# Rank indices converted on VectorE, eight score tiles, and three more U products behind the last scores

## The chip, the cores and the metric

One core of a Trainium2 chip runs the kernel. Its engines are TensorE (PE, matrix products), VectorE (DVE), ScalarE (ACT), GpSimd (POOL), and SyncE (SP), which issues most transfers. Each engine runs its own instructions in a fixed order, and waits on semaphores for the others. The metric is the device time of one execution in microseconds (us).

## What is computed

One layer of an encoder on 512 tokens of 1024 features: a mixer (a linear recurrence and a convolution side by side), then a retrieval layer over 128^2 = 16384 experts of one neuron each. The change touches the retrieval:

```python
s = jnp.einsum("thpc,hpkc->thpk", q, sub_keys)        # 8 heads x 2 halves x 128 keys
s1, i1 = lax.top_k(s[:, :, 0], 16)
s2, i2 = lax.top_k(s[:, :, 1], 16)
cand_s = s1[..., :, None] + s2[..., None, :]          # 16 x 16 pairs
top_s, pos = lax.top_k(cand_s, 16)
idx = take_along_axis(i1 * 128 + i2, pos)             # 16 experts for a token and head
gate = softmax(top_s)
act = gelu(einsum("thkd,td->thk", expert_u[idx], xt))
out = einsum("thk,thkd->td", gate * act, expert_v[idx])
```

## The kernel before

For the first 384 tokens (three blocks of 128) the retrieval is computed densely: for each of 128 groups of 128 experts a **U product** (`dense_u`, all experts of the group against the tokens, then gelu), a multiplication with the gates (zero where an expert isn't chosen), and a **V product** that adds into six sums. The last 128 tokens gather their rows instead. Every float32 product is made of three with split operands: ScalarE makes a high part (`split`, L108, `w_hi`), VectorE or GpSimd subtracts it (L110, `w_lo`), and TensorE adds hi*hi, hi*lo and lo*hi. A U product is 24 matmuls of 384 columns (L478 to L480) into one of two buffers `p_e`; ScalarE's gelu (L487) empties it. `w_hi` and `w_lo` have three buffers each, the loaded tiles five.

The stages that matter here, in order:

- **Ranking** (from 277 to 480 us). For each of 16 half heads `hp` a query product (L587 to L589), its copy `q` on ScalarE (L591), the scores `p_s` on TensorE (L602), their copy `s` on ScalarE (L606), and four times `rank` on VectorE (five instructions for the best 16). After heads 1, 3, 5, 6 and 7 `choose` merges: `ii` (L525) converts the indices to bf16, then sums `cs`, the best 16 of them (`ts`, `pos`), `pa` on VectorE, a softmax on GpSimd and ScalarE (L564, L565), `pf` on ScalarE (L545, a conversion of `pa`), and a lookup of the keys by comparison, product and sums (`eq`, L554 to L562). After the scores of `hp` come `US[hp]` U products; their `w_lo` is GpSimd's. One U product runs ahead of all.
- **Scatter** (from 480 to 662 us). `turned` transposes gates and keys of a block (L638, also into `p_e`), then 24 steps of 16 tokens: VectorE builds one-hot tiles `hot` (L661) and `oa` (L665), TensorE multiplies them (L671, 48 small matmuls a step), ScalarE copies (L674, `stg`), SyncE stores to memory (L675). After a step comes a U product whose `w_lo` is VectorE's, while fewer than 46 of them exist.
- **V part** (from 682 us to the end). The gates are loaded back (L740), U products up to 51 are made with `w_lo` on GpSimd (L763), then a loop over 128 groups makes a V product (L777), weighs (L748 to L752), and makes the U product of 47 groups on.

A U product's result stays in a home until its V product: 8 spare tiles, `HOMES_NOW` homes `w_e` that exist during the ranking, others (`w_f`, `w_g`) only later. So a ranking with 15 homes can hold 23 U products: one early and 22 of `US`. The program's order on each engine is set at build time by a scheduler with the buffers in view; it is not the order of the text alone.

Of the kernel before, what the change touches and what calls it, by code (L numbers as in the profile page):

```python
# [8 lines left out]
F32 = mybir.dt.float32  # L9
# [9 lines left out]
P = 128  # L19
T = 512  # L20
D = 1024
NB = T // P
# [4 lines left out]
NK = 128  # L27
# [33 lines left out]
def tile_kernel(ctx, tc, x, par, wi, bd, kd, mg, wo, wq, keys, u_rows, v_rows, u_t, v_t, fg, ffg, sel, out):  # L61
    nc = tc.nc
# [397 lines left out]
    AHEAD_W = 2  # L460
    EARLY = 1

    US = (0, 0, 0, 1, 1, 2, 1, 2, 1, 2, 1, 2, 1, 2, 1, 5)
    us = {}

    HOMES = AHEAD_U + 1 - 8
    HOMES_NOW = 15

    LAG = AHEAD_U - HOMES - 3
    HOMES_END = 3  # L470
# [46 lines left out]
    def choose(rp, v, i, g, keys_, h0, n):  # L517

        hh = slice(h0, h0 + n)
        vv = v[:, hh].rearrange("p h b t k -> p (h b) t k")  # L520
        m = vv.shape[1]
        shp = [P, m, K]

        ii = rp.tile([P, 2, K, m], BF16, name="ii")
        nc.scalar.copy(ii, i[:, hh].rearrange("p h b t k -> p t k (h b)"))  # L525

        cs = rp.tile([P, m, NCD], F32, name="cs", bufs=1)
        for lo_, ni, nj, c0 in ((0, 4, K, 0), (4, 12, 4, 64)):
            (nc.gpsimd if n > 1 else nc.vector).tensor_tensor(
                cs[:, :, c0:c0 + ni * nj].rearrange("p h (i j) -> p h i j", j=nj),  # L530
                vv[:, :, 0, lo_:lo_ + ni].unsqueeze(3).to_broadcast([P, m, ni, nj]),
                vv[:, :, 1, 0:nj].unsqueeze(2).to_broadcast([P, m, ni, nj]), op=ALU.add)
        ts = rp.tile(shp, F32, name="ts")
        pos = rp.tile(shp, U32, name="pos")
        for h in range(m):
            c2 = rp.tile([P, NCD], F32, name="c2")
            best16(ts[:, h], pos[:, h], cs[:, h], c2)

        pa = rp.tile([P, 5, m, K], U32, name="pa")
        for q, (op, arg) in enumerate(((ALU.logical_shift_right, 4), (ALU.logical_shift_right, 2),  # L540
                                       (ALU.bitwise_and, 15), (ALU.bitwise_and, 12),
                                       (ALU.logical_shift_right, 6))):
            nc.vector.tensor_scalar(pa[:, q], pos, arg, None, op0=op)
        pf = rp.tile([P, 5, m, K], F32, name="pf")
        nc.scalar.copy(pf, pa)  # L545
        pb = rp.tile([P, 2, K, m], BF16, name="pb")
        pbm = pb.rearrange("p t k m -> p t m k")
        nc.vector.scalar_tensor_tensor(pbm[:, 0], pf[:, 1], -12.0, pf[:, 0], op0=ALU.add, op1=ALU.max)
        nc.vector.tensor_mul(pf[:, 3], pf[:, 3], pf[:, 4])
        nc.vector.tensor_sub(pbm[:, 1], pf[:, 2], pf[:, 3])  # L550

        eq = rp.tile([P, 2, K, K * m], BF16, name="eq", bufs=1)
        shp2 = [P, 2, K, K * m]
        nc.vector.tensor_tensor(eq, pb.rearrange("p t k m -> p t (k m)").unsqueeze(2).to_broadcast(shp2),  # L554
                                ioj[:, :, 0:K * m].unsqueeze(1).to_broadcast(shp2), op=ALU.is_equal)
        e4 = eq.rearrange("p t j (k m) -> p (t j) k m", m=m)
        nc.vector.tensor_tensor(e4, e4, ii.rearrange("p t j m -> p (t j) m").unsqueeze(2).to_broadcast([P, 2 * K, K, m]),
                                op=ALU.mult)
        for w in (8, 4, 2):
            nc.vector.tensor_add(eq[:, :, 0:w], eq[:, :, 0:w], eq[:, :, w:2 * w])  # L560
        e1, e2 = (eq[:, :, w].rearrange("p t (k m) -> p t k m", m=m) for w in range(2))
        nc.vector.tensor_add(keys_[:, :, hh].rearrange("p t h b k -> p t k (h b)"), e1, e2)  # L562
        g = merge(g[:, hh])
        nc.gpsimd.tensor_tensor(g, ts, ts[:, :, 0:1].to_broadcast(shp), op=ALU.subtract)  # L564
        nc.scalar.activation(g, g, AF.Exp)  # L565
        den = rp.tile([P, m], F32, name="den")
        nc.vector.tensor_reduce(den, g, axis=AX.X, op=ALU.add)
        nc.vector.reciprocal(den, den)
        nc.gpsimd.tensor_tensor(g, g, den.unsqueeze(2).to_broadcast(shp), op=ALU.mult)

    with ExitStack() as rt:
        kp = rt.enter_context(tc.tile_pool(name="kp", bufs=1, side="right"))
        ky = kp.tile([P, 16, NK], F32, name="ky")
        nc.sync.dma_start(ky, keys)
        rp = rt.enter_context(tc.tile_pool(name="rp", bufs=2, side="right"))
        qp = rt.enter_context(tc.tile_pool(name="qp", bufs=4, side="right"))
        ps_q = rt.enter_context(tc.tile_pool(name="ps_q", bufs=3, space=PSUM))
        ps_s = rt.enter_context(tc.tile_pool(name="ps_s", bufs=3, space=PSUM))
        v16 = kp.tile([P, H, NB, 2, K], F32, name="v16")
        i16 = kp.tile([P, H, NB, 2, K], U32, name="i16")  # L580

        def query(hp):
            hi, lo = split(load(wq[hp].rearrange("p c e -> p (c e)")), nc.gpsimd)
            pq = ps_q.tile([P, T], F32, name="pq")
            for c in range(NC):
                cs = slice(c * P, (c + 1) * P)
                nc.tensor.matmul(pq, hi[:, cs], m_hi[:, c, :], start=(c == 0), stop=False)  # L587
                nc.tensor.matmul(pq, hi[:, cs], m_lo[:, c, :], start=False, stop=False)  # L588
                nc.tensor.matmul(pq, lo[:, cs], m_hi[:, c, :], start=False, stop=(c == NC - 1))  # L589
            q = qp.tile([P, T], F32, name="q", bufs=2)  # L590
            nc.scalar.activation(q, pq, AF.Copy)  # L591
            return q

        for _ in range(EARLY):
            dense_u(len(us), nc.gpsimd)
        qs = [query(0)]
        for hp in range(16):
            if 0 < hp < 15:
                qs.append(query(hp + 1))
            p = ps_s.tile([P, NB, NK], F32, name="p_s")  # L600
            for b in range(NB):
                nc.tensor.matmul(p[:, b, :], qs[hp][:, b * P:(b + 1) * P], ky[:, hp, :], start=True, stop=True)  # L602
            if hp == 0:
                qs.append(query(1))
            s = qp.tile([P, NB, NK], F32, name="s")
            nc.scalar.activation(s, p, AF.Copy)  # L606
            for b in range(NB):
                rank(rp, v16[:, hp // 2, b, hp % 2], i16[:, hp // 2, b, hp % 2], s[:, b])
            for _ in range(US[hp]):
                dense_u(len(us), nc.gpsimd)  # L610
            for h0, n in ((0, 2), (2, 2), (4, 2), (6, 1), (7, 1)):
                if hp == 2 * (h0 + n) - 1:
                    choose(rp, v16, i16, gate_d, key_d, h0, n)
        nc.vector.scalar_tensor_tensor(eidx, key_d[:, 0, :, DB], float(NK), key_d[:, 1, :, DB], op0=ALU.mult, op1=ALU.add)
# [278 lines left out]
```

## Time and profile before

| | |
|---|---|
| median of 3 runs | 1543.34 us (1542.52 to 1551.58) |
| the profiled execution | 1543.64 us, span 1541.5 us |
| TensorE busy | 95% of the span |
| VectorE busy | 80% |
| ScalarE, GpSimd busy | 41% each |
| granted TensorE clock, mean | 0.978 of full speed |
| DMA queue of the loads | 222 MB, 42% of 16 engines' time |

The span is counted from the first to the last instruction; the 2.1 us around it are in the execution's time. Busy shares are means over stages with different limits. In a row of the timeline stand the start, the duration, the engine, the line, the operation, output and inputs, and in brackets the idle time before it and what ended that.

### The profile page before, as it was taken

How to read it: one execution, taken by the hardware profiler on the slowest of the kernel's cores; microseconds unless marked ns; L12 is line 12 of the kernel's file. 1: busy time of each engine (PE TensorE's matmuls, PEld its weight loads, DVE VectorE, ACT ScalarE, POOL GpSimd, SP SyncE). 2: the span in 40 equal slices, each digit the busy share in tenths (PEclk: the TensorE clock that was granted, in tenths of full speed). 3: DMA queues.
4: the chain of work that ended last, by engine and by line, in shares of the span. 5: the costliest groups of instructions: out<-in, count | busy, mean ns of one | idle time of the engine just before them, and what ended most of it. 6: DMA issues, size and time to landing. Idle time of an engine off the chain costs nothing.

```text
span 1541.5 us, 21654 instructions
## 1 busy us (share of the span) xinstructions
PE 1467.7 (95%) x7939; PEld 1289.4 (84%) x7939; DVE 1232.5 (80%) x2267; ACT 626.7 (41%) x926; POOL 625.4 (41%) x378
## 2 busy tenths in 40 slices
PE   5998698999988999999999999999999999999997
PEld 4766467899977899898999999999999999888886
DVE  5998556599999999937777777777777778788887
ACT  5457633344434555433333333333333333333333
POOL 1636542467551000124545545544454444443330
PEclk8999899999998999999999999999999999999999
DMA  6211313233222665588899898999989899889983
GB/s 238 82 55 58 134 69 123 97 109 98 92 95 100 226 212 213 212 259 311 290 334 318 327 340 289 342 305 332 326 318 326 301 348 319 304 310 339 331 290 135
DMA packets 137787, 358.69 MB, mean 233 GB/s; under 512 B 10064, under 2 KB 59472, under 8 KB 134352
## 3 DMA queue, kind: packets, MB, share of 16 engines
q1 hardware_dynamic: 100240, 222.03, 42.0%
q0 software_dynamic: 36864, 134.23, 24.2%
q8 instruction: 62, 1.02, 0.3%
q10 hardware_dynamic: 576, 1.05, 0.2%
q14 instruction: 45, 0.37, 0.1%
HBM read 327.91 MB, written 29.36 MB: 232 GB/s over the span
## 4 chain that ended last, share of the span: by engine, by line
PE 81%; DVE 13%; ACT 3%; issue 1%; POOL 1%; DMA 0%; SPq 0%; DVEq 0%; ACTq 0%; POOLq 0%
PE po L777 34%; PE p_e L478 10%; PE p_e L479 10%; PE p_e L480 10%; PE p_g L671 3%; DVE oa L665 2%; PE pq L587 2%; PE pq L588 2%; PE pq L589 2%; DVE hot L661 1%; PE pz L432 1%; PE pz L431 1%; PE pz L433 1%; PE pz L339 1%; PE pz L340 1%
## 5 line engine op out<-in xcount | busy, mean ns | idle before, releaser
L108 ACT CAST w_hi<-raw_t 128x1024 fp32r<-128x1024 f32 x302 | 315.9, 1050 | 411.6 <-PE p_e L479 266.8
L478 PE MATMUL p_e<-m_hi,w_hi 128*128 128x384 f32 x1024 | 350.7, 342 | 4.4 <-ACT w_e L487 3.5
L480 PE MATMUL p_e<-m_hi,w_lo 128*128 128x384 f32 x1024 | 347.3, 339 | 0.0
L479 PE MATMUL p_e<-m_lo,w_hi 128*128 128x384 f32 x1024 | 346.8, 339 | 0.3 <-DVE m_lo L142 0.3
L110 POOL TENSOR_TENSOR w_lo<-raw_t,w_hi 128x1024 fp32r<-128x1024 f32 x70 | 189.8, 2720 | 349.2 <-ACT w_hi L108 349.2
L110 DVE TENSOR_TENSOR w_lo<-raw_t,w_hi 128x1024 fp32r<-128x1024 f32 x232 | 280.9, 1222 | 13.6 <-ACT w_hi L108 13.4
L693 POOL DMA_INDIRECT g_t<-in_u_rows,eidx x128 | 197.4, 1543 | 214.0 <-DVE g_t L705 170.2
L693 POOL DMA_INDIRECT g_t<-in_v_rows,eidx x128 | 178.7, 1396 | 234.8 <-DVE acc L715 222.1
L777 PE MATMUL po<-w_hi,wt_hi 128*128 128x512 f32 x768 | 240.6, 393 | 0.0
L777 PE MATMUL po<-w_hi,wt_lo 128*128 128x512 f32 x768 | 239.5, 391 | 0.0
L777 PE MATMUL po<-w_lo,wt_hi 128*128 128x512 f32 x768 | 238.8, 390 | 0.0
L478 PEld LDWEIGHTS p_e<-m_hi,w_hi 128*128 128x128 f32 x1024 | 194.5, 190 | 8.3 <-ACT w_e L487 3.9
L479 PEld LDWEIGHTS p_e<-m_lo,w_hi 128*128 128x128 f32 x1024 | 194.5, 190 | 3.5 <-DVE m_lo L142 0.5
L480 PEld LDWEIGHTS p_e<-m_hi,w_lo 128*128 128x128 f32 x1024 | 194.5, 190 | 0.0
L777 PEld LDWEIGHTS po<-w_lo,wt_hi 128*128 128x128 f32 x768 | 144.2, 188 | 32.9
L777 PEld LDWEIGHTS po<-w_hi,wt_lo 128*128 128x128 f32 x768 | 144.3, 188 | 30.5
L705 DVE SCALAR_TENSOR_TENSOR g_t<-g_t,Xg 128x1024 f32<-128x1024 f32 x128 | 152.0, 1222 | 19.0 <-DMA g_t<-in_u_rows,eidx 18.8
L777 PEld LDWEIGHTS po<-w_hi,wt_hi 128*128 128x128 f32 x768 | 143.2, 188 | 24.9
L715 DVE SCALAR_TENSOR_TENSOR acc<-g_t,dots,acc 128x1024 f32<-128x1024 f32 x127 | 162.5, 1279 | 1.7 <-DMA g_t<-in_v_rows,eidx 1.7
L750 ACT CAST wt_hi<-w_f 128x384 fp32r<-128x384 f32 x69 | 35.4, 513 | 182.1 <-PE po L777 182.1
L752 DVE TENSOR_TENSOR wt_lo<-w_f,wt_hi 128x384 fp32r<-128x384 f32 x69 | 38.5, 558 | 73.7 <-ACT wt_hi L750 73.6
L665 DVE TENSOR_TENSOR oa<-hot,trb 128x1024 bf16<-128x1024 bf16 x144 | 92.3, 699 | 0.6
(220 smaller groups left out, 1906.2 us busy)
## 6 DMA issues: line engine op xcount, KB each, us to landing
raw_t<-in_u_t SPq DMA_DIRECT2D x128, 512.0 KB, 6.1
raw_t<-in_v_t SPq DMA_DIRECT2D x128, 512.0 KB, 6.1
scr_g<-stg SPq DMA_DIRECT2D x24, 1024.0 KB, 4.8
g_s<-scr_g SPq DMA_DIRECT2D x16, 1536.0 KB, 14.6
raw_t<-in_wi SPq DMA_DIRECT2D x16, 512.0 KB, 4.2
raw_t<-in_wq SPq DMA_DIRECT2D x16, 512.0 KB, 3.6
raw_t<-in_wo SPq DMA_DIRECT2D x8, 512.0 KB, 3.6
raw_t<-in_kd SPq DMA_DIRECT2D x6, 512.0 KB, 3.5
```

The source lines that it names most:

```text
L108: nc.scalar.copy(hi, t)
L110: eng.tensor_sub(lo, t, f(hi))
L478: nc.tensor.matmul(p, hi[:, cs], m_hi[:, c, :TD], start=(c == 0), stop=False)
L479: nc.tensor.matmul(p, hi[:, cs], m_lo[:, c, :TD], start=False, stop=False)
L480: nc.tensor.matmul(p, lo[:, cs], m_hi[:, c, :TD], start=False, stop=(c == NC - 1))
L665: nc.vector.tensor_tensor(oa[:, q], hot[:, 1], over(2 + q, 1), op=ALU.mult)
L671: nc.tensor.matmul(p[:, t, :], hot[:, 0, g, :, o], oa[:, q, g, :, o], start=(q == 0), stop=(q == 2))
L693: nc.gpsimd.indirect_dma_start(out=t, out_offset=None, in_=rows, in_offset=bass.IndirectOffsetOnAxis(ap=eidx[:, k // K, k % K:k % K + 1], ...
L705: nc.vector.scalar_tensor_tensor(t, t, 1.0, Xg, op0=ALU.mult, op1=ALU.mult, accum_out=dots[:, k:k + 1])
L715: nc.vector.scalar_tensor_tensor(acc, t, dots[:, k:k + 1], acc, op0=ALU.mult, op1=ALU.add)
L752: weighed.append(nc.vector.tensor_sub(wlo, flat(w), f(whi)))
L777: nc.tensor.matmul(po[b][hf], lhs[:, bs], rhs[:, hf * 512:(hf + 1) * 512], start=(i == 0 and n == 0), stop=(i == NK - 1 and n == 2))
```

## The change

Three edits. The conversion of the indices `ii` in `choose` goes from ScalarE to VectorE (five instructions). The score tiles `s` have eight buffers, not four. And `US` puts eight U products behind the scores of the last half head, not five, with 18 homes in the ranking instead of 15 (and 23 `w_f` instead of 26, since `wk2` gets `HOMES - HOMES_NOW - HOMES_END`). As the scatter makes U products up to 46 in all, it then makes 20 and not 23, and its last four steps have none, where the last one had none before.

```diff
-    US = (0, 0, 0, 1, 1, 2, 1, 2, 1, 2, 1, 2, 1, 2, 1, 5)
+    US = (0, 0, 0, 1, 1, 2, 1, 2, 1, 2, 1, 2, 1, 2, 1, 8)
...
-    HOMES_NOW = 15
+    HOMES_NOW = 18
...
-        nc.scalar.copy(ii, i[:, hh].rearrange("p h b t k -> p t k (h b)"))
+        nc.vector.tensor_copy(ii, i[:, hh].rearrange("p h b t k -> p t k (h b)"))
...
-            s = qp.tile([P, NB, NK], F32, name="s")
+            s = qp.tile([P, NB, NK], F32, name="s", bufs=8)
```

What it does to the engines' order is seen at three places. First ScalarE, from the copy of the last scores (`s`) to the gelu of the third product behind them. The products are told apart by the number of their `p_e`: 3818, 3851, 3884 and so on are the first, second and third. Before:

```order
L606 ACTIVATE s_3786<-p_s_3781 128x512
L108 CAST w_hi_3913<-raw_t_3911 128x1024
L487 ACTIVATE w_e_3843<-p_e_3818 128x384
L525 CAST ii_3977<-i16_1905 128x128
L108 CAST w_hi_3946<-raw_t_3944 128x1024
L487 ACTIVATE w_e_3876<-p_e_3851 128x384
L565 ACT_TABLE_LOAD
L565 ACTIVATE gate_d_65<-gate_d_65 128x64
L545 CAST pf_4014<-pa_4008 128x320
L487 ACT_TABLE_LOAD
L487 ACTIVATE w_e_3909<-p_e_3884 128x384
```

And now:

```order
L606 ACTIVATE s_3786<-p_s_3781 128x512
L108 CAST w_hi_3913<-raw_t_3911 128x1024
L487 ACTIVATE w_e_3843<-p_e_3818 128x384
L108 CAST w_hi_3946<-raw_t_3944 128x1024
L487 ACTIVATE w_e_3876<-p_e_3851 128x384
L565 ACT_TABLE_LOAD
L565 ACTIVATE gate_d_65<-gate_d_65 128x64
L545 CAST pf_4113<-pa_4107 128x320
L487 ACT_TABLE_LOAD
L487 ACTIVATE w_e_3909<-p_e_3884 128x384
```

Only `ii` has left; the exponential and `pf` stand where they stood, ahead of the third product's gelu. The merge before this one differs in the same way: there `ii` leaves, and `pf` stays ahead of the copy of the last query.

Second TensorE, at the transposes with which the scatter begins. Before, they follow the fifth product behind the last scores (`p_e_3950`), and the first product of the scatter follows them:

```order
L478 MATMUL p_e_3950<-m_hi_70,w_hi_3946 128x384
L479 MATMUL p_e_3950<-m_lo_71,w_hi_3946 128x384
L480 MATMUL p_e_3950<-m_hi_70,w_lo_3948 128x384
L638 MATMUL p_e_4053<-ident_58,src_4054 128x128
L638 MATMUL p_e_4058<-ident_58,src_4059 128x128
L638 MATMUL p_e_4063<-ident_58,src_4064 128x128
L478 MATMUL p_e_4149<-m_hi_70,w_hi_4145 128x384
```

Now they follow the eighth (`p_e_4049`):

```order
L478 MATMUL p_e_4049<-m_hi_70,w_hi_4045 128x384
L479 MATMUL p_e_4049<-m_lo_71,w_hi_4045 128x384
L480 MATMUL p_e_4049<-m_hi_70,w_lo_4047 128x384
L638 MATMUL p_e_4152<-ident_58,src_4153 128x128
L638 MATMUL p_e_4157<-ident_58,src_4158 128x128
L638 MATMUL p_e_4162<-ident_58,src_4163 128x128
L478 MATMUL p_e_4248<-m_hi_70,w_hi_4244 128x384
```

So 72 matmuls have come between the last scores and the transposes.

Third TensorE at the end of the scatter, around the last small matmul into `p_g_6541`. The five products that follow the scatter (made for homes 47 to 51) write `p_e_6576`, `6609`, `6642`, `6675` and `6708`. Before, all five, 120 matmuls, stand behind it:

```order
L671 MATMUL p_g_6541<-oa_6523,hot_6521 128x128
L671 LDWEIGHTS hot_6521
L671 MATMUL p_g_6541<-oa_6523,hot_6521 128x128
L478 MATMUL p_e_6576<-m_hi_70,w_hi_6572 128x384
L479 MATMUL p_e_6576<-m_lo_71,w_hi_6572 128x384
```

Now the first two and three matmuls of the third have moved in among the last scatter steps, and 69 are left behind it:

```order
L671 MATMUL p_g_6541<-oa_6523,hot_6521 128x128
L671 LDWEIGHTS hot_6521
L671 MATMUL p_g_6541<-oa_6523,hot_6521 128x128
L478 MATMUL p_e_6642<-m_hi_70,w_hi_6638 128x384
L479 MATMUL p_e_6642<-m_lo_71,w_hi_6638 128x384
```

From the first V product on, TensorE's order is the same in both.

## Rows read from the trace of the kernel before

**Rows 1.** Windows: length, busy (instructions) of each engine, clock, DMA share, GB/s.
```profile
440.00:460.00 20.00, 12.61 (x63) 12.29 (x62) 19.47 (x81) 10.30 (x15) 11.70 (x6) 0.83 0.24 80
...
620.00:640.00 20.00, 20.00 (x204) 19.68 (x201) 20.00 (x26) 9.63 (x18) 0.00 (x0) 1.00 0.59 221
```

**Rows 2.** Waits, TensorE and ScalarE, 400 to 480 us: total, times, longest.
```profile
PE p_s L602 <- ACT q L591: 7.4, 1, 7.4
PE p_e L478 <- ACT w_e L487: 3.5, 1, 3.5
...
ACT ii L525 <- DVE i L508: 22.4, 3, 13.1
ACT w_hi L108 <- issue: 12.0, 4, 3.7
ACT gate_d L565 <- POOL gate_d L564: 9.1, 3, 5.0
ACT w_hi L108 <- PE p_e L479: 1.5, 1, 1.5
ACT pf L545 <- DVE pa L543: 1.2, 3, 0.4
```

**Rows 3.** Timeline of ScalarE at the last two merges.
```profile
447.32 0.46 ACT L545 CAST pf<-pa 128x320 f32<-128x320 uint32 x1 [0.39 <-DVE pa L543]
...
448.63 0.59 ACT L591 ACTIVATE q<-pq 128x512 f32<-128x512 f32 x1
...
474.31 0.49 ACT L487 ACTIVATE w_e<-p_e 128x384 f32<-128x384 f32 x1
```

**Rows 4.** Timeline of TensorE from the last scores to the transposes.
```profile
449.27 2.07 PE L602 MATMUL p_s<-ky,q 128*128 128x128 f32 x8 [7.39 <-ACT q L591]
...
456.01 0.33 PE L478 MATMUL p_e<-m_hi,w_hi 128*128 128x384 f32 x1
...
456.53 0.33 PE L478 MATMUL p_e<-m_hi,w_hi 128*128 128x384 f32 x1
...
464.68 0.34 PE L480 MATMUL p_e<-m_hi,w_lo 128*128 128x384 f32 x1
468.56 0.69 PE L478 MATMUL p_e<-m_hi,w_hi 128*128 128x384 f32 x1 [3.55 <-ACT w_e L487]
...
480.75 0.33 PE L638 MATMUL p_e<-ident,src 128*128 128x128 f32 x1 [0.95 <-ACT src L637]
```

**Rows 5.** Timeline of VectorE: a key, a sum, the scatter.
```profile
432.50 0.58 DVE L562 TENSOR_TENSOR key_d<-eq 128x256 f32<-128x256 bf16 x1
...
441.50 0.41 DVE L529 TENSOR_TENSOR cs<-v 128x256 f32<-128x256 f32 x1
...
484.06 2.36 DVE L661 TENSOR_TENSOR hot<-iot,trb 128x2048 bf16<-128x2048 bf16 x2 [0.24 <-ACT trb L639]
...
641.75 3.22 DVE L661 TENSOR_TENSOR hot<-iot,trb 128x2048 bf16<-128x2048 bf16 x1
...
652.04 1.21 DVE L661 TENSOR_TENSOR hot<-iot,trb 128x2048 bf16<-128x2048 bf16 x1
...
656.35 1.89 DVE L665 TENSOR_TENSOR oa<-hot,trb 128x1024 bf16<-128x1024 bf16 x3
```

**Rows 6.** Groups of VectorE, 484 to 659 us: busy, mean ns, idle before.
```profile
L110 DVE TENSOR_TENSOR w_lo<-raw_t,w_hi 128x1024 fp32r<-128x1024 f32 x20 | 24.4, 1218 | 1.5 <-ACT w_hi L108 1.5
```

**Rows 7.** Timeline of GpSimd at the scatter's end.
```profile
641.31 2.58 POOL L110 TENSOR_TENSOR w_lo<-raw_t,w_hi 128x1024 fp32r<-128x1024 f32 x1 [159.34 <-ACT w_hi L108]
```

**Rows 8.** Timeline of ScalarE, VectorE and TensorE from the scatter to V.
```profile
660.39 2.21 ACT L674 ACTIVATE stg<-p_g 128x512 f32<-128x512 f32 x4
...
678.73 0.98 ACT L750 CAST wt_hi<-g_t 128x384 fp32r<-128x384 f32 x2 [2.89 <-DVE g_t L748]
...
678.14 1.03 DVE L748 TENSOR_TENSOR g_t<-g_t,g_s 128x384 f32<-128x384 f32 x2 [19.90 <-DMA g_s<-scr_g]
...
682.66 0.62 PE L777 MATMUL po<-w_hi,wt_hi 128*128 128x512 f32 x2
```

## The prediction

> **What bounds the kernel now.** I read the table of windows first, then the waits, then the rows in order of time around the stretch that the change touches. TensorE is the busiest engine (95% in the table), but not everywhere. From 440 to 460 us it works 12.61 of 20 us while VectorE works 19.47 [rows 1]: at the end of the ranking VectorE sets the pace. In the scatter both are full (20.00 and 20.00 of 20 us) [rows 1].
>
> The waits of TensorE and ScalarE from 400 to 480 us show why TensorE starves [rows 2]. ScalarE waits 22.4 us in all for indices of VectorE (the conversion `ii`), the longest time 13.1 us. TensorE waits twice, 7.4 us for the query `q` of the last scores and 3.5 us for a gelu `w_e`. The rows in time order show what really stands ahead of each. `q` runs at 448.63, behind `pf` at 447.32, and `pf` waits for VectorE's merge as `ii` does [rows 2, 3]. Taking `ii` away leaves `pf`. The last scores start at 449.27 [rows 4]. In what follows product 1 to 5 (after the change 1 to 8) are the U products behind them.
>
> **The conversions on VectorE.** Five go over. No row shows a VectorE conversion of this kind. From below it costs nothing (it could fit where VectorE waits); from above, the nearest row is the 128x256 sum `cs` at 0.41 us [rows 5], so 2 us for five. The three large ones lie well ahead; I take two small ones of 0.3 us on the path, 0.6 us, since they follow `cs` directly in the last two merges. ScalarE gains what it no longer waits: in its order the conversion of product 1's U tile now stands ahead of the first wait and the gelu of product 2 ahead of the second. The first gives TensorE nothing, because its instructions run in order and the last scores, which come first, still wait for `q`. The second lets product 4 run without its wait.
>
> **Eight tiles of scores.** Four more buffers are worth something only where ScalarE waits for a free one. Among ScalarE's waits there is none of that kind [rows 2], and the order does not change. I cost it at nothing; if VectorE fell further behind, it would be cover.
>
> **Three more products behind the last scores.** A product is 24 matmuls; three start every 0.52 us [rows 4], so 4.16 us. Before, products 1 to 3 end at 465.02 [rows 4]; product 4 then waits 3.55 us for a free buffer of sums, that is for the gelu of product 2. It and product 5 take from 468.56 to 479.80 (0.95 us ahead of the first transpose), 11.24 us instead of 8.32, at a lower clock (the granted clock from 440 to 460 us, around the first of these waits, is 0.83 of full speed [rows 1], between the levels of 1.2 and 2.4 GHz): 2.9 us lost. The three transposes of the scatter start at 480.75 [rows 4].
>
> After: product 4 runs from 465.0 to 469.2. Product 5 needs the gelu of product 3, which stands behind the second `pf` and ends at 474.80 [rows 3]; with the 0.6 us, product 5 starts at 475.4. The wait has not gone, it has moved by one product and grown to 6 us. At the clock seen in product 4 it takes 4.16 + 2.9 = 7.1 us, to 482.5; products 6 to 8 take 12.5 us, to 495.0. Then the transposes start: 495.0 against 480.75, **14.25 us later**. VectorE, whose ranks are done by about 481 (before, the first transpose followed them at 480.75), waits for them: its first one-hot comes 3.3 us behind the first transpose, as before (484.06 [rows 5]), at 498.3.
>
> **What the scatter gives back.** VectorE sets its pace: from 484.06 to the end of the last `oa` at 658.24 [rows 5] are 174.2 us, with 20 subtractions `w_lo` of 1.22 us [rows 6]. Three go: 3.7 us less. Against that stand the products after the scatter, whose `w_lo` GpSimd does. A one-hot that meets one takes 3.22 us, not 1.21 [rows 5], and there the two started within 0.5 us of each other [rows 7]. Before, two such subtractions fall into VectorE's work. After, the last five products begin among the last scatter steps, and with three buffers of weights four of the five `w_lo` fall in: two more, 4.0 us. So VectorE needs 174.5 us and ends at 672.8.
>
> The Trainium skill (SBUF — State Buffer, section "SBUF: two separate sides") has a rule for this: GpSimd and a VectorE instruction with two inputs in SBUF hold a shared pair of ports for a whole instruction, and the other blocks. By that rule the trace agrees: the one-hot ended 1.1 us after GpSimd's instruction. Priced as full blocking by that instruction's 2.58 us the two would cost 5.2 instead of 4.0 us.
>
> **The way to the first V product.** Before, the last scatter tile is copied by 662.60, the gates come back from memory at 678.14, and the first V matmul starts at 682.66, after five products that fill the time [rows 8]. It could have started at 679.3: the first of two weights, converted from 678.73 in 0.98 us, is then done [rows 8], 16.7 us behind the copy. After, only 69 of 120 matmuls are left behind the last scatter matmul. VectorE's end at 672.8, 1.2 us of matmuls and 0.6 us of copy give 674.6; 16.7 us more give 691.3. TensorE has run out of products at 674.0 + 12.0 = 686.0 and waits 5.3 us. So the V products start at 691.3 against 682.66, 8.6 us later, and at the lower clock: after its wait of 7.39 us the last scores and three products took 15.75 us (449.27 to 465.02), some 2.2 above their time, after 3.55 us two took 2.9 more; I take 2.5. From there TensorE's order is the same as before and TensorE is full, so that the end moves as much.
>
> Two small terms: the `w_lo` of product 1 now runs just when VectorE forms a key (432.50, [rows 5]), 0 to 2.0 us, and the queue that loads the gates has one more tile load ahead of it that waits for a subtraction, 0 to 1.5 us. I take 1.0 and 0.5.
>
> Sum: 8.6 + 2.5 + 1.0 + 0.5 = **+12.6 us**. The profiled execution took 1543.64 us (span 1541.5), 0.3 above the median of 1543.34. That gives 1556.2; I say **1556**.
>
> In short: the change is (delay of the transposes) + 0.3 - 2.5 - 3.4 + 2.5, and small terms. The 2.5 taken off is that the last scatter matmuls no longer queue behind a product (copy's end +12.0 against VectorE's +14.5), the 3.4 is the slack of the gates (679.3 against 682.66). It breaks even where the transposes are about 3 us late, at 484.
>
> **Rivals.**
> 1. *The three products fill idle time.* If product 5 does not wait for `pf`, products 4 to 8 end at 465.0 + 20.8 = 485.8, the transposes are 5.1 us late and the sum is about +2: 1546. For it speaks that TensorE is idle 11 us in this stretch [rows 2]; against it that ScalarE's order keeps both `pf` ahead of what TensorE needs. Chance 0.10.
> 2. *Not slower: the last scores come early.* If `q` is no longer held, they start when the query is done, about 442, and if the second `pf` holds nothing either, eight products end before 480. Then the transposes wait for the last key only and are not late: -3 us, 1540.5. The point that decides is whether `pf` still stands ahead of `q`; it does. More than 3 us cannot be gained here, since the ranks end at 480 by VectorE. Chance 0.05.
> 3. *More collisions of GpSimd and VectorE.* The key meets `w_lo` fully (+1.0), a fifth `w_lo` falls into the scatter's end (+2.0), the five conversions cost their upper bound on the path (+1.4), the load queue its 1.5 (+1.0), the clock 2.9 (+0.4): +18.4, 1562. The rule cited above would go this way. For it speaks the 3.22 us row; against it that most of these are races. Chance 0.25.
> 4. The forecast, 0.60, by itself 1551 to 1560.
>
> **Numbers.** Within 1% of 1543.3 (15.4 us), about what a measurement of this kernel can tell from no change, lie rivals 1 and 2, most of the forecast and a little of rival 3. Slower by over 1% (above 1558.8): nine tenths of rival 3 (0.22) and the upper part of the forecast (0.11), 0.33. Faster by over 1% needs the transposes 12 us earlier, before the ranks they need exist: 0.02. Same: 0.65. The range reaches from rival 1's side to rival 3: 1545 to 1563.
>
> **What would show it.** In the new profile: the last scores still start at 449 to 452, behind `pf`; TensorE waits for a gelu of about 6 us near 469; the first transpose starts near 495 and VectorE is idle from about 481 to 498 but for three subtractions; the last `oa` ends near 673; TensorE waits some 5 us for the first weights and V starts near 692. I am wrong if the transposes start before 484 (then no loss), if the scatter is more than 3 us shorter than 174, or if the V products run faster than before.

## The result, and the profile after

The changed kernel takes **1561.61 us** (median of 6 runs, 1559.30 to 1562.46) against 1544.30 us of the kernel before in the same comparison (1542.52 to 1551.58). The ratio is **1.0107, 95% interval 1.0092 to 1.0123**: slower by some 17 us, on the edge of the 1% beyond which the prediction called a difference slower. The profiled execution took 1562.46 us with a span of 1560.7 us. The median lies within the predicted range (1545 to 1563), and 5.6 us above the predicted 1556.

Windows of the changed kernel: length, busy time and instructions of TensorE's matmuls, of its weight loads, VectorE, ScalarE and GpSimd, then granted clock, DMA share, GB/s. They answer to [rows 1].

```profile
440.00:460.00 20.00, 10.28 (x51) 9.96 (x50) 19.51 (x91) 5.84 (x9) 6.72 (x4) 0.74 0.09 29
...
620.00:640.00 20.00, 20.00 (x212) 19.53 (x211) 19.88 (x24) 10.50 (x18) 2.52 (x1) 1.00 0.53 204
...
680.00:700.00 20.00, 12.35 (x70) 12.03 (x70) 5.03 (x6) 5.82 (x10) 1.56 (x1) 0.87 0.79 236
700.00:720.00 20.00, 20.00 (x80) 16.38 (x80) 10.09 (x17) 6.54 (x10) 3.20 (x3) 0.88 0.70 224
```

At the end of the ranking TensorE works even less than before (10.28 of 20 us against 12.61), and a new hole has opened at 680 to 700 us, where it works 12.35 us.

Waits of the changed kernel, 400 to 480 us (total, times, longest), to be read beside [rows 2]:

```profile
ACT gate_d L565 <- POOL gate_d L564: 28.7, 3, 15.0
...
PE p_s L602 <- ACT q L591: 9.7, 1, 9.7
...
PE p_e L478 <- ACT w_e L487: 5.5, 1, 5.5
```

ScalarE's 22.4 us of waits for `ii` are gone. In their place it waits 28.7 us for the softmax of the same merges (9.1 us before). TensorE waits longer than before, for the same two tiles. The rows in time order, of ScalarE and then of TensorE, answer to [rows 3, 4]:

```profile
451.68 0.26 ACT L565 ACTIVATE gate_d<-gate_d 128x64 f32<-128x64 f32 x1 [15.04 <-POOL gate_d L564]
452.33 0.46 ACT L545 CAST pf<-pa 128x320 f32<-128x320 uint32 x1 [0.39 <-DVE pa L543]
...
453.64 0.59 ACT L591 ACTIVATE q<-pq 128x512 f32<-128x512 f32 x1
...
476.91 0.26 ACT L565 ACTIVATE gate_d<-gate_d 128x64 f32<-128x64 f32 x1 [8.23 <-POOL gate_d L564]
...
479.33 0.49 ACT L487 ACTIVATE w_e<-p_e 128x384 f32<-128x384 f32 x1
```

```profile
454.28 2.08 PE L602 MATMUL p_s<-ky,q 128*128 128x128 f32 x8 [9.72 <-ACT q L591]
...
479.87 0.69 PE L478 MATMUL p_e<-m_hi,w_hi 128*128 128x384 f32 x1 [5.51 <-ACT w_e L487]
...
498.10 0.27 PE L638 MATMUL p_e<-ident,src 128*128 128x128 f32 x1
```

`q` still stands behind `pf`; the wait for a gelu has moved from product 4 to product 5 (479.87); the transposes start at 498.10 instead of 480.75. VectorE starts its first one-hot at 501.57 (484.06 before [rows 5]) and ends its last `oa` at 678.42 (658.24):

```profile
501.57 2.36 DVE L661 TENSOR_TENSOR hot<-iot,trb 128x2048 bf16<-128x2048 bf16 x2 [0.20 <-ACT trb L639]
...
676.52 1.90 DVE L665 TENSOR_TENSOR oa<-hot,trb 128x1024 bf16<-128x1024 bf16 x3
```

On the way to the first V product, in the order of engines SyncE (its queue), VectorE, TensorE, beside [rows 8]:

```profile
681.59 0.33 SPq L103 DMA_DIRECT2D raw_t<-in_u_t  x1
682.01 0.38 SPq L675 DMA_DIRECT2D scr_g<-stg  x1
...
688.59 6.21 SPq L740 DMA_DIRECT2D g_s<-scr_g  x2
```

```profile
698.54 1.03 DVE L748 TENSOR_TENSOR g_t<-g_t,g_s 128x384 f32<-128x384 f32 x2 [4.29 <-DMA g_s<-scr_g]
```

```profile
699.69 1.22 PE L777 MATMUL po<-w_hi,wt_hi 128*128 128x512 f32 x2 [7.65 <-ACT wt_hi L750]
```

V starts 17.0 us later than before (682.66), and TensorE stands idle for 7.65 us ahead of it. The span grew by 19.2 us in these two executions; 1.84 us of that were there already at the first scores (276.65 and 278.49), ahead of all that the change touches. In the twelve kernels below the first scores lie between 275.58 and 278.89 whatever the edit, so this is taken as a difference between executions (from the first scores on, the two differ by 17.4 us, and the medians by 17.3). Times are given from the first scores where a microsecond matters.

### The profile page after: what moved, and what is told of

Same layout as the page of the kernel before. It is cut to its first block, busy times and chain, and to the rows that moved or that the text cites. A ratio compares the mean times of both kernels' runs of the same rounds, so it can differ in the third digit from the quotient of the medians.

```text
span 1560.7 us, 21647 instructions
## 1 busy us (share of the span) xinstructions
PE 1470.5 (94%) x7939; PEld 1287.0 (82%) x7939; DVE 1244.1 (80%) x2269; ACT 624.9 (40%) x921; POOL 634.6 (41%) x381
## 4 chain that ended last, share of the span: by engine, by line
PE 71%; DVE 22%; ACT 3%; DMA 1%; issue 1%; POOL 1%; SPq 0%; DVEq 0%; ACTq 0%; POOLq 0%
PE po L777 34%; PE p_e L478 9%; PE p_e L479 8%; PE p_e L480 8%; PE p_g L671 2%; DVE oa L665 2%; DVE hot L661 2%; DVE eq L560 2%; PE pz L432 1%; DVE eq L557 1%; PE pz L433 1%; PE pz L431 1%; DVE i L508 1%; DVE s L506 1%; DVE i L505 1%
## 5 line engine op out<-in xcount | busy, mean ns | idle before, releaser
L110 POOL TENSOR_TENSOR w_lo<-raw_t,w_hi 128x1024 fp32r<-128x1024 f32 x73 | 198.0, 2725 | 331.7 <-ACT w_hi L108 320.0
L750 ACT CAST wt_hi<-w_f 128x384 fp32r<-128x384 f32 x60 | 30.8, 513 | 157.6 <-PE po L777 157.6
L665 DVE TENSOR_TENSOR oa<-hot,trb 128x1024 bf16<-128x1024 bf16 x144 | 92.7, 701 | 0.8
L671 PE MATMUL p_g<-oa,hot 128*128 128x128 bf16 x1152 | 82.8, 222 | 6.5 <-DVE oa L665 6.1
```

The source lines that it names most:

```text
L110: eng.tensor_sub(lo, t, f(hi))
L665: nc.vector.tensor_tensor(oa[:, q], hot[:, 1], over(2 + q, 1), op=ALU.mult)
L671: nc.tensor.matmul(p[:, t, :], hot[:, 0, g, :, o], oa[:, q, g, :, o], start=(q == 0), stop=(q == 2))
```

## The experiments

Theory A, the prediction's: three products behind the last scores are paid for, because ScalarE's row holds `q` and then a gelu behind a merge. The rivals asked how much belongs to the conversions, and how much to GpSimd and VectorE meeting. "Before" in a ratio is the kernel before, run beside.

### e1_ii_only: the conversions alone

```
-        nc.scalar.copy(ii, i[:, hh]...)
+        nc.vector.tensor_copy(ii, i[:, hh]...)      # the kernel before, otherwise
```

> The kernel before with one edit: the five conversions ii go from ScalarE to VectorE. The prediction costed this at +0.6 us on the last scores and 0 to 2 us for one key that meets a subtraction of GpSimd, so 1543 to 1546 us. Theory A, from the trace of the changed kernel (three large conversions of 0.96 us, three keys of 2.5 to 2.8 us where before two of them took 0.6): the last scores start 3 to 5 us later than 449.27, so at 452 to 454, the transposes as much later, and the time is 1546 to 1549. Rival B: the later scores of the changed kernel (1.84 us of them there already ahead of the first ranking) have nothing to do with ii, and ScalarE's freed time lets product 4 run without its 3.55 us wait: last scores at 449 to 450, transposes up to 3 us earlier, 1540 to 1543.

Measured: 1546.12 us, ratio 1.0015 (1.0002 to 1.0028). VectorE at the third merge, then TensorE:

```profile
434.12 2.52 DVE L562 TENSOR_TENSOR key_d<-eq 128x256 f32<-128x256 bf16 x1
```

```profile
452.88 2.07 PE L602 MATMUL p_s<-ky,q 128*128 128x128 f32 x8 [9.75 <-ACT q L591]
...
478.47 0.69 PE L478 MATMUL p_e<-m_hi,w_hi 128*128 128x384 f32 x1 [5.55 <-ACT w_e L487]
```

Theory A holds: the last scores come 175.8 us behind the first ones, 3.2 later than before, just as in the changed kernel. The conversions themselves take 0.97 us each in the three large merges, where 0.41 was the upper bound taken, and cost next to nothing: VectorE no longer waits 0.78 us there for GpSimd's sums, and from the first scores `pf` of the first merge is only 0.14 us later. What costs is the key behind it: it takes 2.82, 2.52 and 2.52 us, and before 0.59, 2.69 and 0.58. It now falls into a row of GpSimd's `w_lo` each time (the third of them ends at 436.17, the key at 436.64). The wait of product 4 is gone, product 5 waits 5.55 us, as it does in the changed kernel; with five products that wait is still there.

### e2_s8_only: eight tiles of scores alone

```
-            s = qp.tile([P, NB, NK], F32, name="s")
+            s = qp.tile([P, NB, NK], F32, name="s", bufs=8)
```

> The kernel before with one edit: eight tiles of scores instead of four. Prediction: nothing, 1542 to 1546 us, the scores and the transposes at the same times to 0.5 us. Rival: the scores run further ahead of VectorE, so that ScalarE reaches pf and q in another order of time or the stretch ahead of the ranking is 1.8 us longer as in the changed kernel; then the first scores start at 278.5 instead of 276.65 and the time is about 1545 to 1547.

Measured: 1544.53 us, ratio 1.0006 (0.9991 to 1.0021). From the first scores (275.58) the last ones stand at 172.6 and the first transpose at 204.1, as before. Nothing, as predicted.

### e3_products_only: three more products alone

```
-    US = (..., 1, 2, 1, 5)        HOMES_NOW = 15
+    US = (..., 1, 2, 1, 8)        HOMES_NOW = 18
```

> The kernel before with one edit: three more U products behind the last scores (eight instead of five, 18 homes in the first part). Theory A: nearly the whole loss is here. The last scores stay at 449.3, the wait for the second pf moves behind product 4 and grows, and the transposes start 12 to 15 us later than 480.75, at 493 to 496. By the prediction's way from there (2.5 and 3.4 us given back, 2.5 lost to the clock) 1553 to 1556; by what the changed kernel showed (the delay passed on in full, and 2.5 for the clock) 1556 to 1560. Rival B: without ii on VectorE the three products fit the idle time better, the transposes are less than 8 us late, 1546 to 1551, and the rest of the loss belongs to the conversions.

Measured: 1557.62 us, ratio 1.0082 (1.0047 to 1.0117). TensorE:

```profile
449.51 2.08 PE L602 MATMUL p_s<-ky,q 128*128 128x128 f32 x8 [7.40 <-ACT q L591]
...
468.82 0.69 PE L478 MATMUL p_e<-m_hi,w_hi 128*128 128x384 f32 x1 [3.54 <-ACT w_e L487]
...
492.82 0.27 PE L638 MATMUL p_e<-ident,src 128*128 128x128 f32 x1
```

By the ratios, three quarters of the loss are here. The detail of theory A is wrong for this kernel: with `ii` on ScalarE the wait stays at product 4 (3.54 us). The three products follow 4 and 5 in one piece, and the transposes come 11.8 us later from the first scores; that is the whole cost up to there. The three single edits sum to 1.0015 + 1.0006 + 1.0082, 1.03% in all; the whole change is 1.07%.

### e4_early: the three products ahead of the last scores

```
-    US = (..., 1, 2, 1, 8)        # the changed kernel
+    US = (..., 1, 2, 4, 5)
```

> The changed kernel with one edit: the three extra U products stand ahead of the last scores (four instead of one there) and five behind, as before. Theory A (where a product stands decides; ahead of the last scores TensorE is idle 9.7 us for q): the last scores start some 4 to 6 us later than 454.28, at 458 to 460, behind them five products with the wait of 3 to 6 us, and the transposes start at 489 to 494 instead of 498.1: 1552 to 1558. Rival B: q is held by pf all the same, ScalarE has the gelus of the three products in its row behind pf, so that nothing fills the idle time: transposes at 497 or later, 1560 to 1564.

Measured: 1559.36 us, ratio 1.0087 (1.0054 to 1.0119), whose interval overlaps that of the changed kernel. The transposes start at 492.17, 3.9 us earlier from the first scores, so far as A says. But the last scores start at 466.24, not 458 to 460: the third product ahead of them waits 8.79 us for a gelu (at 455.49), since that gelu stands behind `pf` too. The gain is gone before V: the scatter took 178.8 us (1.9 more) and the way from its last `oa` to V another 2.0 more, and V starts 421.3 us behind the first scores (421.2 in the changed kernel). In time this is inconclusive.

### e7_free: nothing of the merge in ScalarE's way

```
-        nc.scalar.copy(pf, pa)
+        (nc.scalar.copy if n > 1 else nc.vector.tensor_copy)(pf, pa)
...
+        if h0 == 6:
+            return
+        if h0 == 7:
+            hh, ts, m = slice(6, 8), both[0], 2 * m
...
+        with tc.issue_after(gelus[-3].ins) if h0 == 7 else ExitStack():
             nc.scalar.activation(g, g, AF.Exp)
```

(`both` holds `ts` of the last two merges, which get one softmax; `gelus` lists the gelus of the U products; `issue_after` places an instruction behind another in its engine's order.)

> The changed kernel with what held q and the gelus taken out of ScalarE's row: in the last two merges VectorE converts pf itself, and the softmax of both is done once, behind the last merge, its Exp placed behind the gelu of product 6. Theory A (pf and Exp ahead of q and of a gelu are the whole reason why the eight products cost their full time): the last scores start at 442 to 447 instead of 454.28, no wait of TensorE for a gelu over 2 us, the transposes at 482 to 487 instead of 498.1, and since that delay is passed on in full, 1544 to 1551 us. Rival B (the products cost their time wherever they stand, or the clock or the loads hold them): transposes at 493 or later, 1556 to 1561.

Measured: 1562.07 us, ratio 1.0123 (1.0108 to 1.0139). TensorE, then GpSimd (the numbers of lines have moved):

```profile
443.88 1.05 PE L616 MATMUL p_s<-ky,q 128*128 128x128 f32 x8
...
476.53 0.69 PE L481 MATMUL p_e<-m_hi,w_lo 128*128 128x384 f32 x1 [14.61 <-POOL w_lo L110]
```

```profile
450.13 2.40 POOL L110 TENSOR_TENSOR w_lo<-raw_t,w_hi 128x1024 fp32r<-128x1024 f32 x1 [2.40 <-ACT w_hi L108]
473.75 0.40 POOL L577 TENSOR_TENSOR gate_d<-ts 128x128 f32<-128x128 f32 x1 [21.22 <-DVE ts L508]
474.10 7.14 POOL L110 TENSOR_TENSOR w_lo<-raw_t,w_hi 128x1024 fp32r<-128x1024 f32 x3
```

Half of A holds: with `pf` and the Exp out of the way `q` runs at once and the last scores start at 443.88 with no wait. The other half fails: all that was won is lost in one wait of 14.61 us for a `w_lo`, which stands in GpSimd's row behind the softmax's subtraction, and that waits 21.22 us for VectorE's merge. The merge had held the products in two engines; freeing one shows the other. The transposes (495.74, 1.9 us earlier from the first scores) and the time are nearly those of the changed kernel, as rival B's numbers said, though the products did not cost "wherever they stand".

### e7b_free5: the same with five products

```
-    US = (..., 1, 2, 1, 8)        HOMES_NOW = 18        # e7_free; Exp behind the gelu of the last product
+    US = (..., 1, 2, 1, 5)        HOMES_NOW = 15
```

> As e7_free, with five products behind the last scores and 15 homes as before (Exp behind the gelu of product 5). The ranks and keys of VectorE then set the transposes: 480 to 484, TensorE idle 8 to 12 us ahead of them in one piece. 1541 to 1548 us: no gain over the kernel before worth more than 0.2%. Rival (idle time of TensorE ahead of the transposes costs, and it costs more in one piece than in two): 1548 to 1552.

Measured: 1547.95 us, ratio 1.0034 (1.0021 to 1.0047). The same wait stands in product 4 (14.60 us, ending at 475.47), and the transposes wait another 4.44 us for the gates, whose Exp stands behind the last gelu: 486.72 instead of 480 to 484. Slower than before, by GpSimd's row again; the question that this run was to answer, what one long idle time costs, stays open.

### e8_vec: the subtractions behind the scatter on VectorE

```
     while len(us) < AHEAD_U:
-        dense_u(len(us), nc.gpsimd)        # the changed kernel
+        dense_u(len(us), nc.vector)
```

> The changed kernel with one edit: the subtractions w_lo of the five U products that follow the scatter are made by VectorE, not GpSimd. Four of them met a hot or oa of VectorE in the changed kernel (3.0 to 4.0 us instead of 1.2 or less, 8.9 us together) and the last one held a load and with it the last store of the gates by 1.0 us. Theory A (these meetings are why the scatter did not get shorter by its three subtractions): the scatter takes 172 to 174.5 us instead of 176.85, the V products start 3 to 5 us earlier relative to the transposes, 1556 to 1559 us. Rival B (the meetings fall where VectorE had time to spare, TensorE sets the scatter's pace): scatter 176 or more, 1560 to 1563 us.

Measured: **1550.86 us, ratio 1.0059** (1.0044 to 1.0073), against 1.0107 for the changed kernel: well below what A expected. The scatter takes 170.5 us instead of 176.85. To see why, the end of the scatter in the changed kernel, first VectorE, then GpSimd, then TensorE (beside [rows 5, 7]):

```profile
636.91 3.22 DVE L661 TENSOR_TENSOR hot<-iot,trb 128x2048 bf16<-128x2048 bf16 x1
...
655.78 3.03 DVE L661 TENSOR_TENSOR hot<-iot,trb 128x2048 bf16<-128x2048 bf16 x1 [2.37 <-PE p_g L671]
...
670.00 3.42 DVE L661 TENSOR_TENSOR hot<-iot,trb 128x2048 bf16<-128x2048 bf16 x1
```

```profile
636.53 2.52 POOL L110 TENSOR_TENSOR w_lo<-raw_t,w_hi 128x1024 fp32r<-128x1024 f32 x1 [144.77 <-ACT w_hi L108]
...
655.34 2.39 POOL L110 TENSOR_TENSOR w_lo<-raw_t,w_hi 128x1024 fp32r<-128x1024 f32 x1 [9.21 <-ACT w_hi L108]
669.38 2.95 POOL L110 TENSOR_TENSOR w_lo<-raw_t,w_hi 128x1024 fp32r<-128x1024 f32 x1 [11.65 <-PE p_g L671]
```

```profile
646.73 0.22 PE L671 MATMUL p_g<-oa,hot 128*128 128x128 bf16 x1 [2.52 <-DVE oa L665]
...
659.59 0.29 PE L671 MATMUL p_g<-oa,hot 128*128 128x128 bf16 x2 [1.90 <-DVE oa L665]
```

A one-hot that meets a `w_lo` takes 2 us more; TensorE then waits for `oa`; and later VectorE waits 2.37 us for TensorE, which is to give back a tile. The delay is paid twice. The kernel before has one such wait of VectorE for TensorE in its scatter, at the start and not behind a meeting:

```profile
491.14 1.23 DVE L661 TENSOR_TENSOR hot<-iot,trb 128x2048 bf16<-128x2048 bf16 x1 [1.11 <-PE p_g L671]
```

In e8_vec none of these rows is left: TensorE waits 1.2 us for `oa` in the whole scatter (6.1 in the changed kernel, 3.7 before), and its clock from 640 to 680 us is 1.00 instead of 0.91.

The shorter scatter is 6.3 us of a gain that, from the first scores, amounts to 10.6 at the start of V. The rest, 4.3 us, lies between the last copy and V, in SyncE's queue:

```profile
668.55 0.33 SPq L103 DMA_DIRECT2D raw_t<-in_u_t  x1
672.65 0.32 SPq L675 DMA_DIRECT2D scr_g<-stg  x1
...
676.56 5.35 SPq L740 DMA_DIRECT2D g_s<-scr_g  x2
```

The last store of the gates is issued 0.03 us behind its copy; in the changed kernel it came 1.4 us behind it (0.4 before), after a load that waited for a buffer which GpSimd held. And from that store to the first reading of the gates 3.9 us pass, instead of 6.6. In all nine traces here with a tile load issued within 1 us ahead of that store, the kernel before among them, this takes 6.6 to 7.0 us; in the five where the last load was issued 4.1 us ahead it takes 3.9. No run moves the load alone, so that the load is the cause is not shown.

### e9_free_vec: both

```
     e7_free and e8_vec together
```

> e7_free and e8_vec together. If both theories A hold and the two gains add: transposes at 482 to 487, scatter 172 to 174.5, and 1539 to 1547 us, 3 to 5 us below e7_free. If the scatter's end is set by TensorE once its products come earlier: as e7_free, 1544 to 1551.

Measured: 1550.33 us, ratio 1.0043 (1.0030 to 1.0056): e8_vec within the intervals. The wait for GpSimd is there as in e7_free (14.59 us), so e7's edit adds nothing here either; the gain of e8_vec does not need it.

### e10_all_free: the last softmax off GpSimd

```
-        nc.gpsimd.tensor_tensor(g, ts, ...)        # e9_free_vec; the product g * 1/den likewise
+        (nc.gpsimd if n > 1 else nc.vector).tensor_tensor(g, ts, ...)
```

> e9_free_vec with one edit: the subtraction and the product of the last softmax go from GpSimd to VectorE. In e7_free the last scores started at 443.88 as theory A wanted, but product 4 then waited 14.6 us for its w_lo, which stood on GpSimd behind the softmax's subtraction (that waited 21.2 us for ts of VectorE). Theory A (each engine whose row holds a step of the merge ahead of a step of the products makes TensorE wait; free all three and the products fill the idle time): no wait of TensorE over 2 us between the last scores and product 8, transposes at 480 to 486 instead of 493.5, scatter 171 to 173 us, 1535 to 1542 us, so faster than the kernel before. Rival B (GpSimd's subtractions, now running through the last ranks, slow VectorE and so move the keys): last key at 486 or later, transposes 488 or later, 1543 to 1548.

Measured: 1546.81 us, ratio 1.0019 (1.0010 to 1.0028). Its windows at the end of the ranking, then TensorE's first transpose:

```profile
440.00:460.00 20.00, 20.00 (x122) 20.00 (x122) 19.66 (x91) 8.01 (x12) 10.42 (x5) 1.00 0.35 114
460.00:480.00 20.00, 19.14 (x111) 18.82 (x109) 19.80 (x97) 5.59 (x7) 6.99 (x3) 1.00 0.27 87
```

```profile
492.81 0.48 PE L653 MATMUL p_e<-ident,src 128*128 128x128 f32 x1 [13.66 <-ACT w_e L488]
```

The products now fill the idle time: no wait from the last scores to 479.1, where product 8 ends, and a full clock. That much of A is shown. But the transposes still come at 492.81. They need the buffer of sums that the gelu of product 8 empties, and that gelu stands on ScalarE behind the copy of the gates, which waits 7.95 us for VectorE's product of the softmax; this one was placed behind the last key and a `w_lo`. Rival B's numbers fit, its mechanism only in part: the last key is 1.7 us later from the first scores than in the changed kernel, and one of the last two keys meets a `w_lo` (2.58 us instead of 0.38).

### e11_ii_large_act: the large conversions back

```
-        nc.vector.tensor_copy(ii, ...)        # e10_all_free
+        (nc.scalar.copy if n > 1 else nc.vector.tensor_copy)(ii, ...)
```

> e10_all_free with the three large conversions ii back on ScalarE (the two small ones stay on VectorE). By e1_ii_only the conversions on VectorE cost 3.2 us at the last scores. Theory A: the last scores start 2.5 to 3.5 us earlier than in e10_all_free relative to the first ones, the transposes 1 to 3.5 us earlier, 1 to 3.5 us less time in all. Rival B (ScalarE waits longer, holds a gelu again and gives it back to TensorE's waits): no difference from e10_all_free beyond 1 us, or slower.

Measured: 1545.81 us, ratio 1.0014 (1.0005 to 1.0023). From the first scores the last ones come 0.84 us earlier than in e10_all_free, and so does the transpose: less than A wanted. Two of the three large keys meet a `w_lo` here too (2.69 us), since GpSimd's subtractions stand elsewhere than before. So the 3.2 us of e1_ii_only belong, by these rows, less to the conversion than to the places where keys and subtractions come to lie.

### e12_before_vec: the same step of e8 in the kernel before

```
     while len(us) < AHEAD_U:
-        dense_u(len(us), nc.gpsimd)        # the kernel before
+        dense_u(len(us), nc.vector)
```

> The kernel before with one edit: the w_lo of the five U products behind the scatter on VectorE instead of GpSimd (as e8_vec, without the change). Two of them met VectorE's work in the kernel before. Theory A (there TensorE set the way to the first V product: it had products to run until 682.8, 3.4 us past the gates): the scatter is 2 to 4 us shorter, the V products gain no more than 1 us, 1542 to 1545 us. Rival B (the scatter's end decides in both kernels): 1538 to 1541 us.

Measured: **1538.87 us, ratio 0.9971** (0.9959 to 0.9983): faster than both kernels, and A, which took most of the price of the two meetings in the kernel before for hidden, is wrong. Waits of TensorE, 480 to 680 us, then the window in which the meetings lie, each time first of the kernel before and then of this one:

```profile
PE p_g L671 <- DVE oa L665: 3.7, 5, 2.5
```

```profile
PE p_g L671 <- DVE oa L665: 0.8, 3, 0.3
```

```profile
640.00:660.00 20.00, 17.01 (x163) 16.12 (x163) 18.00 (x19) 8.04 (x13) 5.22 (x2) 0.91 0.49 176
```

```profile
640.00:660.00 20.00, 20.00 (x212) 19.53 (x211) 17.10 (x23) 10.48 (x18) 0.00 (x0) 1.00 0.59 216
```

The scatter is 2.5 us shorter and V starts at 678.14 instead of 682.66. From the scatter to V TensorE is full in both kernels, and V waits for its products, as A said; the gates, ready at 672.83, are not what V waits for. But in the kernel before TensorE was late with them, because within the scatter it had waited 2.51 us for one `oa` and had run at a clock of 0.91 from 640 to 660 us. So rival B's time came out, by TensorE's row and not by the scatter's end alone.

### e13_row: three places in the rows

```
-        with tc.issue_after(gelus[-3].ins) if h0 == 7 else ExitStack():
+        with tc.issue_after(gelus[-1].ins) if h0 == 7 else ExitStack():
             nc.scalar.activation(g, g, AF.Exp)
...
+        with tc.issue_after(done.ins) if done else ExitStack():
             last = nc.vector.tensor_add(keys_[:, :, hh].rearrange("p t h b k -> p t k (h b)"), e1, e2)
...
+        with tc.issue_after(last_key[0].ins) if last_key and eng is nc.vector else ExitStack():
             eng.tensor_sub(lo, t, f(hi))
```

(`done` is the softmax's product of the last merge, `last_key` its key.)

> e11_ii_large_act with three places in a row put right. There the eight products ran without a wait, but the transposes stood behind the gelu of product 8, that behind the copy of the gates, and that behind VectorE's product of the softmax, which was placed behind the last key and a w_lo. Now the Exp stands behind the gelu of product 8, the softmax's product ahead of the last key, and VectorE's first w_lo behind that key. Theory A (the rows of the engines are what is left): the first transpose follows the last scores by 42 to 45 us instead of 48.0, so at 482 to 486 when the first scores start near 276, the first one-hot 3 to 5 us earlier relative to the first scores, and the time is 1539 to 1543 us, below e11_ii_large_act and not above the kernel before. Rival B (VectorE's own work from the last scores to the key sets it): first one-hot as in e11_ii_large_act to 1 us, 1544 to 1547.

Measured: 1542.10 us, ratio 0.9990 (0.9981 to 0.9999). TensorE:

```profile
485.89 0.47 PE L660 MATMUL p_e<-ident,src 128*128 128x128 f32 x1 [9.34 <-ACT src L659]
```

A holds in all its numbers: the first transpose 43.7 us behind the last scores, the first one-hot 4.5 us earlier from the first scores than in e11_ii_large_act, and eight products behind the last scores that cost nothing. They gain next to nothing either (0.1%): TensorE idles 9.34 us ahead of the transposes, now for VectorE's merge alone, the bound that rival 2 of the prediction named. It idles another 5.47 us ahead of V (680.00), where it was full in the kernel before: the products that fill one hole are missing in later ones. This kernel has e8's edit in it, which gives the kernel before 0.3% by itself (e12_before_vec): against that, three more products behind the last scores are no gain even where they cost no time of their own.

## Why the prediction was right, and where it was off

The sign, the mechanism and the place were right; the size fell short. Of the signs named, the last `oa` (678.42 instead of 673) and the start of V (699.69 instead of 692) came later than said. The way from the first scores to the end, predicted and measured as differences between after and before:

| step | predicted | measured |
|---|---|---|
| up to the first scores | 0 | +1.84 |
| first scores to last scores | +1.6 | +3.17 |
| last scores to transposes | +13.65 | +12.34 |
| transposes to the first one-hot | 0 | +0.16 |
| scatter on VectorE | +0.3 | +2.67 |
| last `oa` to the last copy | -2.5 | -2.15 |
| last copy to the first V | -2.9 | -1.00 |
| V start to the end of the span | +2.5 | +2.17 |
| sum | +12.65 | +19.20 |

- **The conversions and the keys** (0.6 on the path, and 1.0 for one key). Mis-sized: 3.17, and nearly all of it by keys. That a key meets a `w_lo` was foreseen for one key; two more do than before (e1_ii_only). The 0.41 us taken as the upper bound of a conversion was wrong too (0.96 for the large ones), yet mostly hidden.
- **Eight tiles of scores**: nothing, and e2_s8_only shows it.
- **Three products ahead of the transposes**: right. The wait moved to product 5 and took 5.51 us (6 predicted), and the last scores with four products ran 454.28 to 474.36. The four products behind the wait took 18.2 us, where 19.6 had been taken (granted clock 0.92 from 480 to 500 us; in the kernel before 0.83 from 460 to 480). Without the conversions, e3_products_only, the same three cost 11.8 us without the wait moving. That `pf` stands ahead of `q` and decides was the point on which rival 2 hung; e7_free shows it, and that the same merge sits in GpSimd's row as well, which the prediction did not look at.
- **The scatter** (174.5 us). Mis-sized: 176.85. Four subtractions fell into it, as predicted, and the two additional ones cost 4.7 us where 4.0 was taken (the one-hots together 64.0 us, before 59.7; the `oa` 92.7 and 92.3). The step that failed is "VectorE sets its pace": TensorE, held by the late `oa`, held VectorE in turn for 2.37 us. The kernel before had one such wait, of 1.11 us at the scatter's start, which the changed kernel has not. So this added 1.3 us, and with the 0.7 of the meetings that is 2.0 of the 2.4 us missed. e8_vec removes both, and the scatter falls by 6.3 us, though VectorE makes five more subtractions in it.
- **The slack of the gates** (3.4 us given back, 0.5 for the load queue). Only 1.0 was given back. The store was issued 1.4 us behind its copy (0.4 before), for the queue, and the gates took 9.95 us to be read, where they had taken 8.41. Why the reading took longer is not settled: in e8_vec it took 9.7 and in e12_before_vec 7.9.
- **The clock of V** (2.5 us): right. The first 72 matmuls of V took 19.17 us against 16.64 before, and the end came 2.17 us later than V's start alone makes it.

So what happened is the forecast's mechanism with much of rival 3, more meetings of GpSimd and VectorE, on top: keys, scatter and the way of the gates make up 1.6 + 2.4 + 1.9 = 5.9 of the 6.6 us missed (1.5 of them the slower reading, whose cause is open); the rest is the 1.84 ahead of the change, less 1.1 that the other steps together came out lower. Rival 3 gave 1562, and named the keys and the load queue; the wait of VectorE for TensorE was in neither. That the time fell on its number is in part luck, since its fifth `w_lo` in the scatter did not come, nor its 2.9 us of clock. The Trainium skill (SBUF — State Buffer, section "SBUF: two separate sides"), by whose rule these meetings block for a whole instruction, spoke for that rival; by that rule the traces agree, with keys that took 2.5 us and ended within half a microsecond of GpSimd's row (in e1_ii_only 436.64 against 436.17).

## What to carry to other kernels

Filling an engine's idle time with more work can help only if nothing that the idle time waits for stands in the same rows: look for the late producer (here VectorE's merge) in the order of every engine that feeds the new work, not only the one named by the wait, and find out what else will then be last, and where the work that was moved will be missed. The places where a long GpSimd subtraction meets VectorE can be worth more than the edit that shifts them; take the price of each meeting with the wait of the third engine that it causes. Moving five such subtractions to the engine that they block was the edit that gained most here, apart from taking the three products back: 0.3% in the kernel before, and nearly half a per cent in the changed one, part of it by an earlier store and not by fewer meetings.

## What was not expected of the hardware

A conversion on VectorE with one input was blocked like those with two: `pf`, 128x320 from uint32 to f32, took 0.33 us alone and 2.38 us beside GpSimd's `w_lo` (e7_free, 479.04, GpSimd's row ending at 481.24). The conversion `ii` on VectorE took 0.96 us for 256 elements a partition and 0.26 us for 128, so nearly four times as long for twice the size; its order of reading differs between the two (two heads or one), and which part of that costs was not tried. After TensorE's idle 7.65 us the granted clock was 0.88 over the next 20 us, and 72 matmuls of V took 2.5 us longer; in e10_all_free, with no hole from 440 to 479 us, it was 1.00 throughout.
